# Delta heads of a hybrid decoder layer: PSUM banks shared out anew, and the weight sums' transfers placed elsewhere

## The chip, the cores and the metric

The kernel runs on one core of a Trainium2 chip. The metric is the time of one execution on the device in microseconds. A core has a matrix engine (TensorE, PE in the profile, with its weight loads as PEld), a vector engine (VectorE, DVE), a scalar engine (ScalarE, ACT) and a general one (GpSimd, POOL). SyncE (SP) only issues transfers (DMAs) here. Matmuls write to PSUM. In the stage that is changed the kernel's pools hold eight PSUM tiles of up to 2 KB in each of 128 partitions, one bank to a tile.

## The reference, cut to what matters

One layer over 512 tokens of width 2048, in float32. A projection feeds two branches: attention in a sliding window, and gated DeltaNet, a recurrence with one state S per head. Their outputs are gated, added and multiplied by `w_out`. DeltaNet has 16 key heads, 32 value heads (two to a key head) and heads of 128 channels.

```python
proj = h @ w_in
aq, ak, av, ag, d_qkv, dz, db, da, mg_a, mg_b = jnp.split(proj, _split_points(), axis=-1)
...
d_qkv = causal_conv_silu(d_qkv, conv_w)          # 4 taps
dq, dk, dv = jnp.split(d_qkv, [DN_KEY, 2 * DN_KEY], axis=-1)
...
o = gated_delta_rule(dq, dk, dv, g, beta)
o = rms_norm(o, dn_norm_w) * jax.nn.silu(dz.reshape(B, T, DN_V_HEADS, DN_HEAD_V).astype(f32))
y_b = o.reshape(B, T, DN_VAL).astype(x.dtype) @ w_o_dn
y = jax.nn.sigmoid(mg_a) * y_a + jax.nn.sigmoid(mg_b) * y_b
return x + gate * (y @ w_out)

def gated_delta_rule(q, k, v, g, beta):
    ...
    def step(S, xs):
        u_c, w_c, qk_c, qd_c, kd_c, gl_c = xs
        v_new = u_c - w_c @ S
        o = qd_c @ S + qk_c @ v_new
        S = S * gl_c[..., None, None] + jnp.swapaxes(kd_c, -1, -2) @ v_new
        return S, o
```

## The kernel before, in words

**Products.** A float32 product is made of three faster ones: both factors are split into a high and a low part, and `mm3` (L255 to L257) adds hi x hi, hi x lo and lo x hi in one PSUM tile of 128x512 (`mm`). For each half of a weight tile ACT casts the high part (`whi`, L61) and DVE subtracts for the low one (`wlo`, L62). A channel tile, 128 channels of the projection, is 16 such triples, 48 matmuls. The output products (of `w_od` and `w_out`) are made in a form with 7 block products instead of 8, which needs sums of weight blocks. Those sums are made early, by `weight_sums` (L1181), and stored in the DRAM tensors `g_d` and `f_d`: there are 24 sets, and each loads four tiles of 128x1024 (512 KB each; tags q00, q10, q11, q01, one buffer each; L1193), makes four sums on DVE (L1197) and stores them (L1199). A tile can be loaded anew only when the store that reads it has ended.

**Stages.** By the profile's times: start up to some 150 us, keys of DeltaNet and attention up to about 1066 us, the delta heads to about 2195 us, then the output products.

**Delta heads.** For each of the 16 key heads (a group g, `heads`, L802) five channel tiles are multiplied, 240 large matmuls: q, v0, v1, z0 and z1. Beside them runs the small work of the same group and the ones before:
- `values`: the conv (L604, then L609 and L611) gives `yv`, four transposes bring it to a PSUM tile `ptv`, and ACT copies that to `vt` (L829).
- `queries`: the conv gives `yq`, which is transposed (`ptq`). For each of two value heads a matrix of decays E is made: a row is loaded from `g_rows` (L737, on SP's queue), masked on POOL (L742), and put through exp on ACT (L748). Then come, each in a PSUM tile of the pool `ptph`: `pqk` (L884), `py` (L892, copied to Y by DVE) and two `pu` (L898 and L899).
- `scan` (L913): four steps c over blocks of 128 tokens. `pp` (L923) multiplies the state S by the keys; DVE makes `r` (L926); `pv` (L933) gives the new values, which ACT copies (`vn`, L935) and DVE scales (`vs`, L940); `pd` (L948) is the update of the state, `po` (L951, L952) the output. ACT copies `po` to `osb` (L953) and squares it twice for the norm (L956); DVE makes the new S from `pd` (L960 in the first step, L963 in the next ones). The next step's `pp` needs that S.
- the end of `scan`: DVE makes the norm (`ms`, the root, and `osb` times it, L982), PE transposes the two heads to `pto`, DVE multiplies that by the gates (`zh`, L989), and the results are stored in `o_d` (L993).

The small tiles `pp`, `pv`, `po` and `pd` come from the pool `psch`, the transposes, `pqk`, `py` and `pu` from `ptph`, the channel tiles from `pmmh`. A pool gives its buffers in turn; who writes a buffer next waits for the readers of what it held.

**What sets the order.** All of this is written as generators that are stepped by `pump` (L90), called once for each two triples, that is six matmuls. A generator started by `go` that yields n waits n pumps. One started by `paced` has a budget: so many units are added at each pump, and a yield of x costs x units. `behind` (L259) ties an instruction to the place of the last large matmul in the order, with no wait on the chip. A scheduler then fixes the order of each engine's instructions, which that engine works off one after the other. An instruction that waits holds up all that stand behind it on its engine. All DMAs are issued by SP, in one such order: weight loads (`raw`, L213), sums, rows of decays, results.

## Time and profile before

| | |
|---|---|
| median of 3 runs | 2892.16 us (2882.42 to 2896.01) |
| the profiled execution, its own time | 2893.1 us |
| its span in the profile | 2891.3 us |
| mean granted clock of TensorE | 0.995 |
| PE, delta heads (1066 to 2195 us): busy | 1113.63 of 1129.00 us, 5837 instructions |
| DVE, there | 731.21 us |
| ACT, there | 430.33 us |
| POOL, there | 78.16 us |
| bytes moved, there | 209 GB/s |

A row of the profile's groups of instructions gives the line, the engine, the operation, what is written and read (`out<-in`, buffer numbers left out), the shapes and the count, then the busy time with the mean of one in ns, then the idle time of the engine just before them and what ended it. A row of the waits view says who waited for whom: total, times, longest. A row of the timeline has the start, the length, the engine (SPq is SP's queue), the line, the instruction and, in brackets, the idle time before it with what ended it. A clock of 1.00 is TensorE's full speed.

### The profile page before, as it was taken

Reading aid. Unit: us, or ns where it says so; the run is one execution under the profiler, and the core shown is the slowest. Engines: PE = TensorE matmul, PEld = TensorE weight load, DVE = VectorE, ACT = ScalarE, POOL = GpSimd, SP = SyncE. Lnnn points to the kernel's source line nnn. Section 1 sums busy time; section 2 is a strip of 40 time slices with the busy share of each in tenths; the row PEclk is TensorE's granted clock in tenths of the full one; section 3 lists DMA queues with packets and bytes.
Section 4 is the critical chain, followed back from the end, with each engine's and each line's share of the span. In section 5 each row is a group of like instructions: output and inputs, shape, how many; then the busy total and the mean of one; then the engine's idle time right before and its main releaser. Section 6 shows DMA issues by size and latency. Waiting matters only on the chain.

```text
span 2891.3 us, 38617 instructions
## 1 busy us (share of the span) xinstructions
PE 2829.9 (98%) x14396; PEld 2320.6 (80%) x14396; DVE 1969.2 (68%) x3174; ACT 1189.4 (41%) x2382; POOL 138.4 (5%) x124
## 2 busy tenths in 40 slices
PE   7899999999999999999999999999999999999999
PEld 5687888877877778888788888888888788878887
DVE  6776786768768666767766666666656766664666
ACT  4356453334444343343433333333334444433343
POOL 0001010100001000100100000000000000000000
PEclk9999999999999999999999999999999999999999
DMA  9777774322252253335777677777746887885684
GB/s 383 292 256 223 242 248 142 114 89 86 83 158 82 108 161 129 121 111 174 255 260 243 233 245 252 241 237 248 242 151 221 279 307 264 298 278 175 245 318 166
DMA packets 227727, 604.27 MB, mean 209 GB/s; under 512 B 76082, under 2 KB 102194, under 8 KB 187090
## 3 DMA queue, kind: packets, MB, share of 16 engines
q1 hardware_dynamic: 227538, 601.81, 62.1%
q8 instruction: 113, 1.85, 0.3%
q14 instruction: 76, 0.61, 0.1%
HBM read 481.32 MB, written 118.17 MB: 207 GB/s over the span
## 4 chain that ended last, share of the span: by engine, by line
PE 84%; DMA 6%; DVE 5%; ACT 2%; issue 1%; POOL 0%; SPq 0%; DVEq 0%; POOLq 0%; ACTq 0%
PE mm L255 20%; PE mm L257 19%; PE mm L256 19%; PE m L256 5%; PE m L255 5%; PE m L257 5%; DMA g_d<-q 2%; DMA E<-g_rows 2%; DVE wlo L62 1%; PE S L1388 1%; DVE wa L437 1%; PE O L1439 1%; ACT whi L61 1%; PE pP L296 1%; PE pv L933 1%
## 5 line engine op out<-in xcount | busy, mean ns | idle before, releaser
L255 PE MATMUL mm<-hh,whi 128*128 128x512 f32 x2784 | 1132.3, 407 | 2.9 <-ACT mth L285 2.8
L257 PE MATMUL mm<-hh,wlo 128*128 128x512 f32 x2784 | 1091.5, 392 | 0.0
L256 PE MATMUL mm<-hl,whi 128*128 128x512 f32 x2784 | 1089.1, 391 | 0.0
L62 DVE TENSOR_TENSOR wlo<-raw,whi 128x1024 fp32r<-128x1024 f32 (+1 forms) x532 | 653.9, 1230 | 470.7 <-ACT whi L61 458.2
L61 ACT CAST whi<-raw 128x1024 fp32r<-128x1024 f32 (+1 forms) x532 | 555.3, 1045 | 867.1 <-PE mm L256 625.3
L255 PEld LDWEIGHTS mm<-hh,whi 128*128 128x128 f32 x2784 | 524.7, 188 | 114.6 <-issue 9.2
L257 PEld LDWEIGHTS mm<-hh,wlo 128*128 128x128 f32 x2784 | 523.7, 188 | 113.9 <-issue 0.5
L256 PEld LDWEIGHTS mm<-hl,whi 128*128 128x128 f32 x2784 | 525.2, 189 | 100.8 <-issue 1.4
L748 ACT ACTIVATE E<-E,neg_g 128x128 f32<-128x128 f32 x256 | 82.2, 393 | 103.5 <-POOL E L742 96.1
L1197 DVE TENSOR_TENSOR q<-q,q 128x1024 f32<-128x1024 f32 x96 | 121.0, 1261 | 0.1
L777 DVE TENSOR_TENSOR atmp<-A 128x62 f32<-128x62 f32 (+30 forms) x124 | 108.9, 878 | 0.5
L785 DVE TENSOR_TENSOR A<-A,atmp 128x62 f32<-128x62 f32 (+30 forms) x124 | 108.1, 872 | 0.5
L880 POOL TENSOR_TENSOR qe<-qe,yq 128x512 f32<-128x512 f32 x32 | 52.7, 1664 | 939.1 <-DMA qe<-eg_rows 809.0
L953 ACT COPY osb<-po 128x256 f32<-128x256 f32 x64 | 23.8, 372 | 153.0 <-PE po L952 153.0
L742 POOL TENSOR_SCALAR_AFFINE_SELECT E<-E 128x512 f32<-128x512 f32 x64 | 54.8, 868 | 448.4 <-DMA E<-g_rows 373.2
L1412 ACT ACTIVATE sm<-sm,mx,rs 128x256 f32<-128x256 f32 (+1 forms) x128 | 71.7, 562 | 3.5 <-DVE mx L1407 3.5
L935 ACT COPY vn<-pv 128x256 f32<-128x256 f32 x64 | 23.8, 372 | 119.5 <-PE pv L933 119.5
L604 DVE SCALAR_TENSOR_TENSOR yv<-mm,convh,yv 128x511 f32<-128x511 f32 (+2 forms) x96 | 71.1, 741 | 1.0
L940 DVE TENSOR_SCALAR vs<-vn,kd 128x128 f32<-128x128 f32 x96 | 23.1, 283 | 57.6 <-ACT vn L935 57.6
L926 DVE SCALAR_TENSOR_TENSOR r<-pp,neg_eg,vt 128x128 f32<-128x128 f32 x96 | 29.1, 344 | 40.6 <-PE pp L923 40.5
L437 DVE SCALAR_TENSOR_TENSOR wa<-wa,silu_cb 128x2048 f32<-128x2048 f32 x24 | 54.8, 2282 | 0.0
L952 PE MATMUL po<-vn,E 128*128 128x128 f32 x256 | 46.8, 275 | 0.0
(427 smaller groups left out, 3662.4 us busy)
## 6 DMA issues: line engine op xcount, KB each, us to landing
raw<-in_w_ch SPq DMA_DIRECT2D x158, 1024.0 KB
wa<-in_w_ada_ss SPq DMA_DIRECT2D x32, 1024.0 KB
q<-in_w_od SPq DMA_DIRECT2D x64, 512.0 KB
g_d<-q SPq DMA_DIRECT2D x64, 512.0 KB
raw<-g_d SPq DMA_DIRECT2D x32, 1024.0 KB
raw<-in_w_od SPq DMA_DIRECT2D x24, 1024.0 KB
gw<-in_w_ada_gate SPq DMA_DIRECT2D x16, 1024.0 KB
E<-g_rows SPq DMA_DIRECT2D x64, 256.0 KB
```

The source lines that it names most:

```text
L61: self.nc.scalar.copy(out=hi, in_=src)
L62: self.nc.vector.tensor_tensor(out=lo, in0=src, in1=hi.bitcast(F32), op=ALU.subtract)
L255: nc.tensor.matmul(ps, lhsT=wh, rhs=xh, start=first, stop=False)
L256: nc.tensor.matmul(ps, lhsT=wh, rhs=xl, start=False, stop=False)
L257: self.last_mm = nc.tensor.matmul(ps, lhsT=wl, rhs=xh, start=False, stop=last)
L437: nc.vector.scalar_tensor_tensor(out=wa, in0=wa, scalar=0.5, in1=scb, op0=ALU.mult, op1=ALU.mult, accum_out=t[:, j : j + 1])
L604: nc.vector.scalar_tensor_tensor(out=y[:, s:], in0=ps[:, : T - s], scalar=w[:, j : j + 1], in1=y[:, s:], op0=ALU.mult, op1=ALU.add)
L748: self.nc.scalar.activation(E[:, c, :], E[:, c, :], AF.Exp, bias=self.neg_g[:, c, h : h + 1])
L777: eng.tensor_tensor(out=t, in0=A[:, m : m + 1, m + 1 :].to_broadcast([P, m, n]), in1=A[:, :m, m : m + 1].to_broadcast([P, m, n]), op=ALU.mult,
L785: self.behind(eng.tensor_tensor(out=A[:, :m, m + 1 :], in0=A[:, :m, m + 1 :], in1=t, op=ALU.add))
L1197: self.behind(nc.vector.tensor_tensor(out=q[f], in0=q[x], in1=q[y], op=ALU.add))
L1412: nc.scalar.activation(t, t, AF.Exp, scale=r[:, h : h + 1], bias=mx[:, h : h + 1], accum_out=den[:, h : h + 1])
```

## The change

In `psch` three buffers stay of four, and `ptph` has three instead of two; the sum stays eight. `po` and `pd` become the two halves of one tile, `pod`. `pp` and `pv` are given the same size, and only half of each is used. The transposes `pto` are written one pump later (`yield 3`). The weight sums begin one group earlier, with 2.0 units per pump for 1.75. Each of their loads is tied to the last large matmul, with one unit between loads and 8.0 units behind the last; each sum is followed by 6.0 units for 4.0, the 2.0 units behind each store go, and 7.0 units stand behind a set. Lines from L1194 on stand one line further down in the changed kernel (the sums are L1198, their stores L1200).

```diff
--- before.py
+++ after.py
@@ -651,8 +651,8 @@
         tc, nc = self.tc, self.nc
         with ExitStack() as sb:
             self.pmm = sb.enter_context(tc.tile_pool(name="pmmh", bufs=2, space=PSUM, reuse_waits="tile"))
-            self.ptp = sb.enter_context(tc.tile_pool(name="ptph", bufs=2, space=PSUM, reuse_waits="tile"))
-            self.psc = sb.enter_context(tc.tile_pool(name="psch", bufs=4, space=PSUM, reuse_waits="tile"))
+            self.ptp = sb.enter_context(tc.tile_pool(name="ptph", bufs=3, space=PSUM, reuse_waits="tile"))
+            self.psc = sb.enter_context(tc.tile_pool(name="psch", bufs=3, space=PSUM, reuse_waits="tile"))
             self.gwk = sb.enter_context(tc.tile_pool(name="gwkh", bufs=1, reuse_waits="tile"))
             wk = sb.enter_context(tc.tile_pool(name="dnB", bufs=2, reuse_waits="tile"))
             self.tt = []
@@ -665,8 +665,8 @@
             ws = sb.enter_context(tc.tile_pool(name="wsum", bufs=1, reuse_waits="tile"))
             sums = None
             for g in range(KH):
-                if g == 4:
-                    sums = self.paced(self.weight_sums(ws), 1.75)
+                if g == 3:
+                    sums = self.paced(self.weight_sums(ws), 2.0)
                 if g == 8:
                     self.drain_slow(self.solves)
                 self.heads(wk, g)
@@ -919,7 +919,7 @@
         S = None
         for c in range(NTB):
             if c:
-                pp = self.psc.tile([P, 2, P], F32, tag="sc", name="pp")
+                pp = self.psc.tile([P, 4, P], F32, tag="sc", name="pp")[:, 0:2, :]
                 nc.tensor.matmul(pp, lhsT=kT[:, sl(c)], rhs=S, start=True, stop=True)
                 r = wk.tile([P, 2, P], F32, tag="r", name="r", bufs=1)
                 for e in range(2):
@@ -928,7 +928,7 @@
                         in1=v[e][:, c, :], op0=ALU.mult, op1=ALU.add,
                     )
                 yield 2
-            pv = self.psc.tile([P, 2, P], F32, tag="sc", name="pv")
+            pv = self.psc.tile([P, 4, P], F32, tag="sc", name="pv")[:, 0:2, :]
             for e in range(2):
                 nc.tensor.matmul(pv[:, e, :], lhsT=TT[e][:, c, :], rhs=r[:, e, :] if c else v[e][:, c, :], start=True, stop=True)
             vn = wk.tile([P, 2, P], F32, tag="vn", name="vn", bufs=2)
@@ -942,9 +942,9 @@
                         scalar2=None, op0=ALU.mult,
                     )
             yield 1
-            po = self.psc.tile([P, 2, P], F32, tag="sc", name="po")
+            pod = self.psc.tile([P, 4, P], F32, tag="sc", name="pod")
+            po, pd = pod[:, 0:2, :], pod[:, 2:4, :]
             if c < NTB - 1:
-                pd = self.psc.tile([P, 2, P], F32, tag="sc", name="pd")
                 nc.tensor.matmul(pd, lhsT=k[:, c, :], rhs=vs, start=True, stop=True)
             for e in range(2):
                 if c:
@@ -982,7 +982,7 @@
             nc.vector.tensor_tensor(
                 out=of, in0=of, in1=ro[:, e * NTB : (e + 1) * NTB].unsqueeze(2).to_broadcast([P, NTB, P]), op=ALU.mult
             )
-        yield 2
+        yield 3
         for e in range(2):
             pt = self.ptp.tile([P, T], F32, tag="tp", name="pto")
             self.transpose4(pt, lambda c: osb[:, e, c, :])
@@ -1190,14 +1190,15 @@
                         q = []
                         for c, r in ((0, 0), (1, 0), (1, 1), (0, 1)):
                             t = wk.tile([P, 1024], F32, tag=f"q{c}{r}", name=f"q{c}{r}", bufs=1)
-                            nc.sync.dma_start(out=t, in_=w[2 * c + n, 2 * r + i][:, cols])
+                            self.behind(nc.sync.dma_start(out=t, in_=w[2 * c + n, 2 * r + i][:, cols]))
                             q.append(t)
-                        yield 10.0
+                            yield 1.0
+                        yield 8.0
                         for f, (x, y) in enumerate(((0, 1), (1, 2), (0, 2), (2, 3))):
                             self.behind(nc.vector.tensor_tensor(out=q[f], in0=q[x], in1=q[y], op=ALU.add))
-                            yield 4.0
+                            yield 6.0
                             self.behind(nc.sync.dma_start(out=dst[n, f, i][:, cols], in_=q[f]))
-                            yield 2.0
+                        yield 7.0
 
     def rope_tables(self, wk, keep):
         nc, a = self.nc, self.a
```

DVE's order in the third step of the scan of group 11. `wlo` is half of a weight tile, `yq` the q tile of the next group; PE_49 and the like are semaphores of engines and of DMAs. Before:

```order
L940 TENSOR_SCALAR vs<-vn,kd 128x128 [waits Activation_49]
L940 TENSOR_SCALAR vs<-vn,kd 128x128
L62 TENSOR_TENSOR wlo<-raw,whi 128x1024 [waits DMAHW4_49,PE_49,Activation_49]
L963 SCALAR_TENSOR_TENSOR S<-S,egl,pd 128x128 [waits PE_49]
L963 SCALAR_TENSOR_TENSOR S<-S,egl,pd 128x128
L604 SCALAR_TENSOR_TENSOR yq<-mm,convh,yq 128x511 [waits Activation_49,Pool_49]
L604 SCALAR_TENSOR_TENSOR yq<-mm,convh,yq 128x510 [waits DVE_49]
L604 SCALAR_TENSOR_TENSOR yq<-mm,convh,yq 128x509 [waits DVE_49]
L611 SCALAR_TENSOR_TENSOR yq<-th,yq 128x512 [waits Activation_49]
L926 SCALAR_TENSOR_TENSOR r<-pp,neg_eg,vt 128x128 [waits PE_49]
```

The same place of the changed kernel:

```order
L940 TENSOR_SCALAR vs<-vn,kd 128x128 [waits DVE_49,Activation_49]
L940 TENSOR_SCALAR vs<-vn,kd 128x128
L62 TENSOR_TENSOR wlo<-raw,whi 128x1024 [waits DMAHW6_49,PE_49,Activation_49]
L604 SCALAR_TENSOR_TENSOR yq<-mm,convh,yq 128x511 [waits Activation_49,Pool_49]
L604 SCALAR_TENSOR_TENSOR yq<-mm,convh,yq 128x510 [waits DVE_49]
L604 SCALAR_TENSOR_TENSOR yq<-mm,convh,yq 128x509 [waits DVE_49]
L963 SCALAR_TENSOR_TENSOR S<-S,egl,pod 128x128 [waits PE_49,Activation_49]
L963 SCALAR_TENSOR_TENSOR S<-S,egl,pod 128x128
L611 SCALAR_TENSOR_TENSOR yq<-th,yq 128x512 [waits Activation_49]
L926 SCALAR_TENSOR_TENSOR r<-pp,neg_eg,vt 128x128 [waits PE_49]
```

S moved behind the three conv instructions, and it waits for ACT as well as for PE. In eight of the sixteen groups the third step reads so.

PE's order at `py`, group 5 (`lab` and `ta` are blocks from DRAM). Before:

```order
L256 MATMUL mm<-hl,whi 128x512
L257 MATMUL mm<-hh,wlo 128x512
L892 MATMUL py<-ta,lab 64x64 [waits DMAHW5_49,DMAHW4_49,Activation_49]
L892 MATMUL py<-ta,lab 64x64 [waits DMAHW2_49,DMAHW1_49]
L892 MATMUL py<-ta,lab 64x64 x6
L255 MATMUL mm<-hh,whi 128x512
```

The same place of the changed kernel:

```order
L256 MATMUL mm<-hl,whi 128x512
L257 MATMUL mm<-hh,wlo 128x512
L892 MATMUL py<-ta,lab 64x64 [waits DMAHW6_49,DMAHW0_49,DVE_49]
L892 MATMUL py<-ta,lab 64x64 [waits DMAHW2_49,DMAHW1_49]
L892 MATMUL py<-ta,lab 64x64 x6
L255 MATMUL mm<-hh,whi 128x512
```

Nothing moved; the engine that `py` waits for is DVE in place of ACT, since the bank that it takes held `pto` (read for `zh`) and not `ptv` (read for `vt`).

SP's order around the loads of E for group 6. Before:

```order
L859 DMA qe<-eg_rows 128x512 [waits DMAHW2_49,PE_49,Pool_49]
L1193 DMA q_12346<-in_w_od 128x1024 [waits DMAHW4_49,DMAHW3_49]
L1199 DMA g_d<-q_12026 128x1024 [waits DVE_49]
L1193 DMA q_12348<-in_w_od 128x1024 [waits DMAHW5_49,DMAHW0_49]
L737 DMA E<-g_rows 128x512 [waits DMAHW6_49]
L1193 DMA q_12350<-in_w_od 128x1024 [waits DMAHW7_49,DMAHW4_49]
L993 DMA o_d<-zh 128x512 [waits DVE_49]
L993 DMA o_d<-zh 128x512 [waits DMAHW1_49,DVE_49]
L213 DMA raw<-in_w_ch 128x2048 [waits DMAHW2_49,Activation_49]
L737 DMA E<-g_rows 128x512 [waits DMAHW3_49,PE_49]
```

The changed kernel:

```order
L865 DMA tt_9185<-ts_d 64x4x64 [waits DMAHW4_49,PE_49]
L213 DMA raw<-in_w_ch 128x2048 [waits DMAHW5_49,DVE_49]
L1200 DMA g_d<-q_12127 128x1024 [waits DMAHW6_49]
L859 DMA qe<-eg_rows 128x512 [waits DMAHW7_49,PE_49,Pool_49]
L859 DMA qe<-eg_rows 128x512 [waits DMAHW0_49,PE_49,Pool_49]
L737 DMA E<-g_rows 128x512 [waits DMAHW1_49]
L737 DMA E<-g_rows 128x512 [waits DMAHW2_49,PE_49]
L1200 DMA g_d<-q_12143 128x1024 [waits DMAHW3_49,DVE_49]
```

Both loads of E follow the loads of `qe`, where loads and stores of the sums and the stores of `zh` stood between.

## The prediction

> **What bounds the kernel now.** I read the page first, then the stages, then the waits of TensorE in the stage that the change touches.

> ```profile
> span 2891.3 us, 38617 instructions
> ...
> PE 2829.9 (98%) x14396; PEld 2320.6 (80%) x14396; DVE 1969.2 (68%) x3174; ACT 1189.4 (41%) x2382; POOL 138.4 (5%) x124
> ...
> L1197 DVE TENSOR_TENSOR q<-q,q 128x1024 f32<-128x1024 f32 x96 | 121.0, 1261 | 0.1
> ```

> TensorE is busy for 98% of the span, so it is the bound, and what it does is not changed: no matmul goes or comes. The change can only move the time in which TensorE waits, and the time in which it runs at a lower clock. The stages view of the delta heads (1066 to 2195 us) and of two places in it says how much there is (columns: stretch, its length, busy time of PE, PEld, DVE, ACT and POOL with counts, granted clock, DMA share, GB/s):

> ```profile
> 1066.00:2195.00 1129.00, 1113.63 (x5837) 926.01 (x5835) 731.21 (x1187) 430.33 (x997) 78.16 (x62) 1.00 0.64 209
> 1440.00:1445.00 5.00, 2.76 (x12) 1.90 (x11) 4.18 (x4) 2.62 (x6) 2.35 (x1) 1.00 0.99 379
> 1445.00:1450.00 5.00, 4.30 (x24) 3.51 (x25) 3.08 (x4) 1.92 (x6) 0.64 (x1) 0.50 1.13 384
> 1450.00:1455.00 5.00, 5.00 (x32) 3.75 (x31) 2.25 (x5) 1.68 (x2) 0.00 (x0) 0.81 0.87 244
> 1917.00:1922.00 5.00, 4.43 (x24) 3.74 (x25) 5.00 (x7) 2.00 (x5) 0.00 (x0) 1.00 0.27 104
> ```

> PE is idle for 1129.0 - 1113.6 = 15.4 us of this stage. At 1445 the clock falls to half and stays there into the next stretch: 5 x 0.50 + 5 x 0.19 = 3.4 us of work are lost, though PE counts as busy. In the last row, where PE waited too, it stays at 1.00. Who was waited for (total us, times, longest), from 1070 to 2190 us:

> ```profile
> PE py L892 <- ACT vt L829: 5.5, 3, 2.9
> PE pto L296 <- DVE osb L982: 4.4, 3, 2.1
> PE ptv L296 <- DVE yv L611: 2.0, 2, 1.3
> PE ptv L296 <- DVE zh L989: 1.9, 1, 1.9
> PE pv L933 <- DVE r L926: 0.4, 1, 0.4
> PE pp L923 <- DVE S L963: 0.2, 1, 0.2
> ```

> That is 14.4 us of waits, and 17.8 us with the lower clock: 0.6% of the kernel. This is the most that the change can win where it works. The longest wait, in order of time, on SP's queue, POOL, ACT and PE (start, length, instruction, idle time before it):

> ```profile
> 1433.28 0.33 SPq L1193 DMA_DIRECT2D q<-in_w_od  x1
> 1433.66 0.45 SPq L737 DMA_DIRECT2D E<-g_rows  x1
> ...
> 1439.02 3.33 POOL L742 TENSOR_SCALAR_AFFINE_SELECT E<-E 128x512 f32<-128x512 f32 x1 [1.45 <-DMA E<-g_rows]
> 1442.38 1.28 ACT L748 ACTIVATE E<-E,neg_g 128x128 f32<-128x128 f32 x4 [8.67 <-POOL E L742]
> ...
> 1443.57 1.03 ACT L61 CAST whi<-raw 128x1024 fp32r<-128x1024 f32 x1
> ...
> 1445.08 0.56 ACT L829 COPY vt<-ptv 128x512 f32<-128x512 f32 x1
> 1445.70 1.11 PE L892 MATMUL py<-ta,lab 64*64 64x64 f32 x15 [2.94 <-ACT vt L829]
> ```

> The rows of decays (E), issued right behind a load of the weight sums, land 5 us later; POOL waits for them, ACT 8.67 us for POOL, and behind ACT's exponentials stand a cast and the copy vt, which frees the bank that py is to write. PE needs nothing of the late E here (it belongs to the next group); it waits for a bank. And SP's queue, which issues E, is late itself:

> ```profile
> SPq L1193 <- DMA g_d<-q: 113.1, 37, 8.1
> SPq L1199 <- DVE q L1197: 82.5, 38, 7.4
> SPq L1193 <- DMA f_d<-q: 57.0, 17, 7.2
> ```

> Loads of the weight sums wait on SP, up to 8.1 us each, until the store that still reads their tile has ended, and all that stands behind them waits too.

> **The change part by part.** *Third bank (ptph 2 to 3).* In the order of before, py waits for ACT; in the changed order it waits for DVE, that is for zh, two transposes earlier. The waits of 5.5 us go, and the lower clock that follows the longest of them: 5.5 + 3.4 = 8.9 us. The cover is the next user of a bank, pu, 12 matmuls later, which now waits for vt. From 1899.88 to 1900.11 (rows below) a matmul takes 0.23 us, so vt has 12 x 0.23 = 2.8 us more, against a longest wait of 2.9. If E lands as late as at 1439, the win of that one wait is near its 2.8 us all the same, but if it comes later, pu waits instead; ends of this term: 3 to 8.9 us. I take 8.9, since the loads of E also come forward.

> *Sums held behind the matmuls and spread.* The loads of a set come 7 units of 2.0 per pump after its last store, 3.5 pumps, where there were 2 units of 1.75; a pump is six matmuls, 6 x 0.23 = 1.4 us, so the last store has 4.8 us before the next loads begin, where it had 2 / 1.75 x 1.4 = 1.6 us. SP mostly finds its tiles free. In the changed order both E stand straight behind qe in most groups; the second E for group 10 still stands behind the stores of zh, and those of three groups behind one store of sums. The 96 sums on DVE (1261 ns each) and the 192 DMAs stay as many. By itself this is the cure of the late E; its worth is in the other terms.

> *One pump more before pto (yield 3).* The three waits of 4.4 us are those in which sums and casts stand inside the chain of small instructions before osb:

> ```profile
> 1909.61 1.23 DVE L1197 TENSOR_TENSOR q<-q,q 128x1024 f32<-128x1024 f32 x1
> 1910.83 1.22 DVE L62 TENSOR_TENSOR wlo<-raw,whi 128x1024 fp32r<-128x1024 f32 x1
> 1916.82 1.29 DVE L982 TENSOR_TENSOR osb<-osb,roy 128x512 f32<-128x512 f32 x2
> 1917.57 0.66 PE L296 MATMUL pto<-ident,osb 128*128 128x128 f32 x4 [2.09 <-DVE osb L982]
> ```

> A pump of 1.4 us covers the two shorter ones (2.3 us together) and 1.4 of the 2.1: 3.7 us; all 4.4 where no sum (1.2 us) falls into the chain. I take 4.2. What was hidden behind the transposes, the stores of o_d, moves by 1.4 us; nobody but SP's order waits for them.

> *The waits of ptv.* The rows of the two longest:

> ```profile
> 1235.28 0.63 PE L296 MATMUL ptv<-ident,yv 128*128 128x128 f32 x4 [1.35 <-DVE yv L611]
> ...
> 1648.60 0.68 DVE L611 SCALAR_TENSOR_TENSOR yv<-th,yv 128x512 f32<-128x512 f32 x1
> 1649.20 0.68 DVE L989 TENSOR_TENSOR zh<-pto,zh 128x512 f32<-128x512 f32 x1
> ```

> The 1.9 us were spent on the second zh, which ptv no longer needs: it needs yv, 0.6 us earlier. Of the 2.0 us for yv, 1.3 lie at 1235 us, where no sum was made yet, and stay. I leave two waits of 0.7 us (2.0 - 1.3) more or less as they are: 3.9 us become 2.7, 1.2 us won. The ends: 0, and 2.6 if only the 1.3 is left.

> *One bank for po and pd.* This is the part that can cost. The state S (DVE) may now read its half only after ACT has read the other half three times, and its wait stands ahead of wlo, r and the conv on DVE's queue. The third step of a scan, now:

> ```profile
> 1896.23 0.60 PE L948 MATMUL pd<-vs,k 128*128 128x256 f32 x2
> 1899.88 0.39 PE L256 MATMUL mm<-hl,whi 128*128 128x512 f32 x1
> 1900.11 0.39 PE L257 MATMUL mm<-hh,wlo 128*128 128x512 f32 x1
> 1900.34 0.59 PE L923 MATMUL pp<-S,kT 128*128 128x256 f32 x2
> 1895.93 1.22 DVE L62 TENSOR_TENSOR wlo<-raw,whi 128x1024 fp32r<-128x1024 f32 x1 [1.35 <-ACT whi L61]
> 1897.07 0.60 DVE L963 SCALAR_TENSOR_TENSOR S<-S,egl,pd 128x128 f32<-128x128 f32 x2
> 1897.59 2.31 DVE L604 SCALAR_TENSOR_TENSOR yq<-mm,convh,yq 128x511 f32<-128x511 f32 x3
> 1898.61 0.19 ACT L956 ACTIVATION_READ_ACCUMULATOR junk<-po 128x1 f32 x1
> ```

> ACT is done at 1898.61 + 0.19 = 1898.80; S could end at 1899.40, and pp wants it at 1900.34: 0.9 us to spare. But in eight of the sixteen groups the changed order puts all three conv instructions ahead of S here. They would start at 1897.07 and end at 1899.38; S ends 0.60 later, at 1899.98. So 0.36 us are left, less what a signal takes; say 0.3. I take 0 for the term. The ends: nothing, or one wlo more (1.2 us) ahead of S in the third steps of 15 groups, 15 x (1.2 - 0.3) = 14 us. [...]

> The sum: 8.9 + 4.2 + 1.2 = 14.3 us. The profiled execution took 2893.1 us, 1.8 more than its span, and the median of the three runs is 2892.2, so no correction is needed: 2893.1 - 14.3 = 2878.8, say 2879 us, 0.46% less. With the better ends of the terms for pto and ptv (4.4 and 2.6) it is 2877, with the worse ones (3.7 and 0) 2881; 2 us either way for the scatter make the forecast's own bounds 2875 to 2883.

> **The rivals.** *E stays late.* The loads of the sums still stand ahead of some E, 2 MB of them, and E lands behind them; the waits of py move to pu or ptv. For it: the row at 1433.66, right behind one such load. Against: most E stand before them now. Left is pto (4.2) and 3 of the 8.9: 2893 - 7 = 2886.

> *The scan pays.* The 14 us above are paid: 2893, no change. It decides at 0.3 us of delay in the third step. Against it: of the 48 states that pp needs (three to a group), one came late so far, by 0.2 us (the waits of PE).

> *All waits go.* 17.8 us and no residue: 2875.

> *A sum waits for its load, slower than before.* The loads are no longer issued far ahead: the first sum of a set comes 5.5 pumps, 7.6 us, behind the second load, which it needs. A sum that waits holds DVE, and behind it S, r and wlo. There are 24 sets (96 sums, four to a set); past the 0.9 us to spare each costs what it waits. At 2.2 us: 24 x 1.3 = 31 us, 2879 + 31 = 2910; it makes the kernel slower by over 0.5% from 2.1 us on. For it: a store of 512 KB was waited for up to 8.1 us. Against: SP runs ahead of the place at which a load is written, and the sums waited 0.1 us in all so far (first view).

> *The clock.* With three banks for a scan instead of four, short waits follow each other; if one in each group brought the clock down as at 1445, 16 x 3.4 = 54 us: 2879 + 54 = 2933. Against: after the wait of 2.09 the clock stayed at 1.00, and over the whole stage its mean is 1.00. [...]

> **How the numbers follow.** The forecast (2875 to 2883) has 0.58, E late 0.13, the scan pays 0.08, all waits go 0.09, a sum waits 0.08, the clock 0.04. A measurement of this kernel tells about 0.5% from no change, 14.5 us, so the line is at 2878 us, inside the forecast's own bounds. I put half of that case on each side: faster 0.29 + 0.09 = 0.38; the same 0.29 + 0.13 + 0.08 = 0.50; slower 0.08 + 0.04 = 0.12. The range goes from 2872 (all waits gone, and 3 us for the scatter of the runs, which lay between 2882 and 2896) to 2892, and leaves out the slower cases and half of the scan's.

> **What would show it.** Right: in the waits of PE no row py from vt and none for pto over 1 us, the clock at 1.00 in every stretch of the heads, the SP row "L1193 <- DMA g_d<-q" far below 113 us, PE busy unchanged within 4 us. Wrong: new rows "pp <- S" or "pu <- vt" of several us, a row of DVE in which the sum waits for a DMA, or a second fall of the clock.

## The result, and the profile after

The changed kernel takes 2872.93 us in the median of 8 runs (2871.02 to 2877.28). Over 8 runs the kernel before has a median of 2887.82 us, so the ratio is 0.9946, with a 95% interval from 0.9934 to 0.9958. That is 14.9 us less. The forecast was 2879 us, 14.3 us less than the execution that it started from; 2872.93 lies below the forecast's own bounds of 2875 to 2883 and inside the stated range, 2872 to 2892. First the page of the changed kernel's profiled execution (2872.0 us), then the stages view of the delta heads, before and after, from the first matmul of the stage to the first one behind it:

```profile
span 2870.2 us, 38671 instructions
...
PE 2820.4 (98%) x14396; PEld 2314.6 (81%) x14396; DVE 1969.6 (69%) x3174; ACT 1188.4 (41%) x2382; POOL 141.6 (5%) x124
```

```profile
1064.89:2195.56 1130.67, 1114.74 (x5840) 926.95 (x5841) 732.84 (x1189) 431.13 (x999) 78.16 (x62) 1.00 0.64 209
```

```profile
1060.10:2176.38 1116.28, 1110.47 (x5841) 924.74 (x5841) 733.83 (x1189) 431.17 (x999) 80.47 (x62) 1.00 0.63 212
```

The stage is 14.39 us shorter, with the same work on every engine. The two spans differ by 21.1 us, but 4.8 of that lie ahead of the stage (it starts at 1060.10 for 1064.89) and 1.9 behind it, where nothing was changed; the last section comes back to the 4.8. What follows compares the stage. The waits of PE in it, after the change:

```profile
PE pv L933 <- DVE r L926: 2.5, 1, 2.5
PE ptv L296 <- DVE yv L611: 0.7, 1, 0.7
PE pu L898 <- DVE Y L894: 0.6, 1, 0.6
PE pod L948 <- DVE vs L940: 0.3, 1, 0.3
PE pp L923 <- DVE S L960: 0.2, 1, 0.2
```

They sum to 4.3 us, for 14.4. The rows of py and pto are gone, and so is the half clock in the stage (3.4 us): 10.1 + 3.4 = 13.5 of the 14.4 us. One of the signs named for being right did not come: PE's busy time was to stay within 4 us, and it fell by 9.5 us on the page and by 4.3 us in the stage, because the time at half clock counts as busy (before, from 1445 to 1450 us, 4.30 of 5.00 us at a clock of 0.50). On SP's queue the loads of the sums wait far less for their stores (the stores wait longer for the sums, 107.8 us for 82.5):

```profile
SPq L1200 <- DVE q L1198: 107.8, 40, 6.2
...
SPq L1193 <- DMA g_d<-q: 25.6, 8, 4.9
SPq L1193 <- DMA f_d<-q: 6.9, 2, 4.8
```

The part that could cost is the state in the shared bank. The third step of the same scan as in the prediction (start, length, instruction):

```profile
1880.22 0.60 PE L948 MATMUL pod<-vs,k 128*128 128x256 f32 x2
...
1881.05 2.31 DVE L604 SCALAR_TENSOR_TENSOR yq<-mm,convh,yq 128x511 f32<-128x511 f32 x3
...
1882.59 0.19 ACT L956 ACTIVATION_READ_ACCUMULATOR junk<-pod 128x1 f32 x1
...
1883.28 0.60 DVE L963 SCALAR_TENSOR_TENSOR S<-S,egl,pod 128x128 f32<-128x128 f32 x2
...
1884.32 0.59 PE L923 MATMUL pp<-S,kT 128*128 128x256 f32 x2
```

ACT is done with the bank at 1882.78, the three conv instructions on DVE end at 1883.36, S ends at 1883.88 and pp starts at 1884.32: 0.44 us to spare. Where no conv stands ahead of S, 0.87 to 0.90 us are left in most groups (1.08 in most first steps). With a bank of its own the state had 2.40 to 2.86 us in nearly all steps of the kernel before, so the change took 1.3 to 2.2 us of room, and it cost next to nothing: pp waited once in 48 steps, 0.2 us.

The longest wait that is left:

```profile
1400.25 2.02 ACT L790 COPY atmp<-A 64x1024 f32<-64x1024 f32 x1 [2.50 <-DMA ta_d<-atmp]
...
1402.18 1.04 ACT L61 CAST whi<-raw 128x1024 fp32r<-128x1024 f32 x1
...
1403.25 1.22 DVE L62 TENSOR_TENSOR wlo<-raw,whi 128x1024 fp32r<-128x1024 f32 x1 [4.86 <-ACT whi L61]
1404.39 0.60 DVE L926 SCALAR_TENSOR_TENSOR r<-pp,neg_eg,vt 128x128 f32<-128x128 f32 x2
...
1404.79 0.75 PE L933 MATMUL pv<-r,tt 128*128 128x128 f32 x4 [2.49 <-DVE r L926]
```

A copy of the triangular solves holds ACT for 2 us, the cast behind it comes late, wlo behind that, and r stands behind wlo in DVE's order.

### The profile page after: what moved, and what is told of

Same layout as the page of the kernel before. It is cut to its first block, busy times and chain, and to the rows that moved or that the text cites. A ratio compares the mean times of both kernels' runs of the same rounds, so it can differ in the third digit from the quotient of the medians.

```text
span 2870.2 us, 38671 instructions
## 1 busy us (share of the span) xinstructions
PE 2820.4 (98%) x14396; PEld 2314.6 (81%) x14396; DVE 1969.6 (69%) x3174; ACT 1188.4 (41%) x2382; POOL 141.6 (5%) x124
## 4 chain that ended last, share of the span: by engine, by line
PE 87%; DVE 5%; DMA 3%; ACT 2%; issue 1%; SPq 0%; POOL 0%; DVEq 0%; POOLq 0%; ACTq 0%
PE mm L255 20%; PE mm L257 20%; PE mm L256 20%; PE m L256 5%; PE m L255 5%; PE m L257 5%; DVE wa L437 1%; DVE wlo L62 1%; PE pv L933 1%; DMA E<-g_rows 1%; PE S L1389 1%; PE pod L952 1%; PE O L1440 1%; PE pP L296 1%; ACT sm L1413 1%
## 5 line engine op out<-in xcount | busy, mean ns | idle before, releaser
L257 PE MATMUL mm<-hh,wlo 128*128 128x512 f32 x2784 | 1089.5, 391 | 0.0
L256 PE MATMUL mm<-hl,whi 128*128 128x512 f32 x2784 | 1086.9, 390 | 0.0
L62 DVE TENSOR_TENSOR wlo<-raw,whi 128x1024 fp32r<-128x1024 f32 (+1 forms) x532 | 655.2, 1232 | 425.0 <-ACT whi L61 409.6
L61 ACT CAST whi<-raw 128x1024 fp32r<-128x1024 f32 (+1 forms) x532 | 555.4, 1045 | 848.6 <-PE mm L256 612.2
L257 PEld LDWEIGHTS mm<-hh,wlo 128*128 128x128 f32 x2784 | 522.6, 188 | 113.6 <-issue 0.5
L256 PEld LDWEIGHTS mm<-hl,whi 128*128 128x128 f32 x2784 | 524.0, 188 | 100.4 <-issue 1.4
L1198 DVE TENSOR_TENSOR q<-q,q 128x1024 f32<-128x1024 f32 x96 | 124.5, 1297 | 0.2 <-DMA q<-in_w_od 0.2
L748 ACT ACTIVATE E<-E,neg_g 128x128 f32<-128x128 f32 x256 | 82.1, 393 | 88.7 <-POOL E L742 88.6
L953 ACT COPY osb<-pod 128x256 f32<-128x256 f32 x64 | 23.8, 372 | 149.9 <-PE pod L952 149.9
L742 POOL TENSOR_SCALAR_AFFINE_SELECT E<-E 128x512 f32<-128x512 f32 x64 | 60.0, 950 | 430.7 <-DMA E<-g_rows 307.2
L604 DVE SCALAR_TENSOR_TENSOR yv<-mm,convh,yv 128x511 f32<-128x511 f32 (+2 forms) x96 | 71.4, 743 | 1.2
L963 DVE SCALAR_TENSOR_TENSOR S<-S,egl,pod 128x128 f32<-128x128 f32 x64 | 19.3, 343 | 50.8 <-ACT junk L956 50.8
L609 ACT ACTIVATE th<-yv 128x512 f32<-128x512 f32 x32 | 20.1, 628 | 72.7 <-DVE yv L604 72.7
```

What stands on the lines that cost most here:

```text
L61: self.nc.scalar.copy(out=hi, in_=src)
L62: self.nc.vector.tensor_tensor(out=lo, in0=src, in1=hi.bitcast(F32), op=ALU.subtract)
L256: nc.tensor.matmul(ps, lhsT=wh, rhs=xl, start=False, stop=False)
L257: self.last_mm = nc.tensor.matmul(ps, lhsT=wl, rhs=xh, start=False, stop=last)
L604: nc.vector.scalar_tensor_tensor(out=y[:, s:], in0=ps[:, : T - s], scalar=w[:, j : j + 1], in1=y[:, s:], op0=ALU.mult, op1=ALU.add)
L748: self.nc.scalar.activation(E[:, c, :], E[:, c, :], AF.Exp, bias=self.neg_g[:, c, h : h + 1])
```

## The experiments

All are read by the length of the stage of the heads, from its first matmul to the first one behind it. The table gives that length, PE's waits in it (between 1070 and 2170 us), the work lost to the half clock there, and the measured median. Each ratio is to executions of the kernel before that were taken beside it (medians of 2887.8 to 2888.4 us). A stage's length comes from one profiled execution, and the whole times of these lie up to 6 us from their medians, so a difference of a few us between two stages is shown only where the runs agree with it.

| kernel | stage us | waits | half clock | median us | ratio (95% interval) |
|---|---|---|---|---|---|
| before | 1130.7 | 14.4 | 3.4 | 2887.82 | 1 |
| the change | 1116.3 | 4.3 | 0 | 2872.93 | 0.9946 (0.9934 to 0.9958) |
| sums only | 1119.1 | 5.3 | 1.7 | 2873.21 | 0.9951 (0.9935 to 0.9967) |
| banks only | 1123.3 | 8.8 | 1.7 | 2880.15 | 0.9967 (0.9957 to 0.9978) |
| pump only | 1150.7 | 28.3 | 8.5 | 2902.18 | 1.0043 (1.0030 to 1.0056) |
| sums and banks | 1120.7 | 7.0 | 1.7 | 2876.33 | 0.9956 (0.9939 to 0.9974) |
| sums and pump | 1129.2 | 13.9 | 1.7 | 2887.35 | 0.9998 (0.9987 to 1.0009) |
| rhythm, loads untied | 1117.3 | 4.3 | 0 | 2876.39 | 0.9956 (0.9943 to 0.9970) |
| loads tied, old rhythm | 1124.2 | 10.6 | 1.7 | 2880.39 | 0.9973 (0.9961 to 0.9984) |
| change, sums 4 pumps later | 1128.5 | 14.1 | 1.7 | 2888.95 | 0.9998 (0.9986 to 1.0009) |
| change, sums 6 pumps later | 1115.0 | 3.9 | 0 | 2872.75 | 0.9947 (0.9929 to 0.9964) |
| change, copies on POOL | 1118.4 | 5.0 | 1.7 | 2875.88 | 0.9959 (0.9944 to 0.9974) |

### The parts one by one

The sums alone, that is this part of the change on the kernel before:

```diff
-                if g == 4:
-                    sums = self.paced(self.weight_sums(ws), 1.75)
+                if g == 3:
+                    sums = self.paced(self.weight_sums(ws), 2.0)
...
+                            yield 1.0
+                        yield 8.0
...
-                            yield 4.0
+                            yield 6.0
...
+                        yield 7.0
```

> Only the weight sums are placed as in the change; banks and the pump are as before. Theory A, the prediction's: each part has its own term, and the sums alone are worth little: py still waits for vt by 3 us or more, pto for osb by about 4.4, PE's waits in the heads stay at 12 to 14 us, ratio 0.998 to 1.000. Theory B: the late E, and sums that stand in the way, are the source of nearly all, and their new places alone take it away: waits in the heads at most 5 us, ratio 0.994 to 0.997.

```profile
PE ptv L296 <- DVE yv L611: 2.6, 3, 1.7
PE pv L933 <- DVE r L926: 2.4, 1, 2.4
PE pd L948 <- DVE vs L940: 0.3, 1, 0.3
```

Neither py nor pto waits, with two banks in ptph and without the pump. Theory A falls: the sums alone bring 11.6 of the stage's 14.4 us. By the runs they can't be told from the whole change at all (2873.21 and 2872.93 us).

The banks alone:

```diff
-            self.ptp = sb.enter_context(tc.tile_pool(name="ptph", bufs=2, space=PSUM, reuse_waits="tile"))
-            self.psc = sb.enter_context(tc.tile_pool(name="psch", bufs=4, space=PSUM, reuse_waits="tile"))
+            self.ptp = sb.enter_context(tc.tile_pool(name="ptph", bufs=3, space=PSUM, reuse_waits="tile"))
+            self.psc = sb.enter_context(tc.tile_pool(name="psch", bufs=3, space=PSUM, reuse_waits="tile"))
...
+            pod = self.psc.tile([P, 4, P], F32, tag="sc", name="pod")
+            po, pd = pod[:, 0:2, :], pod[:, 2:4, :]
```

> Only the banks (third for ptph, three for psch, po and pd in one tile); the sums and the pump are as before. Theory A: the row py from vt is gone and the half clock with it, pto (4.4) and ptv (about 3.9) stay: about 9 us less, ratio 0.996 to 0.998. Theory B: E is as late as before and the wait for vt moves to pu or ptv, with a row of 3 us or more: ratio 0.998 to 1.000.

The row of py is gone here too, pto stays at 4.5, ptv at 2.6, and pp (1.1) and pu (0.6) are new. 7.4 us of the stage were won. By themselves the banks do about what the prediction said (7.4 us for 8.9); they are no use for what the sums already took away, as the next run shows.

The change without the pump (`yield 2` ahead of pto, as before), so sums and banks:

> The change without the pump ahead of pto (yield 2). Theory A: the row pto from osb is back at 3.5 to 4.4 us, ratio about 0.996. Theory B: pto waits under 1.5 us, since the sums lie elsewhere, ratio 0.9946 as the whole change.

pto waits once, 0.8 us, ptv 3.2 and pv 2.7. Of the two theories that is B's row for pto; but the stage is 4.4 us longer than the change's, 2.7 by waits and 1.7 by a half clock. The runs don't confirm that difference: their intervals overlap (0.9939 to 0.9974, and 0.9934 to 0.9958). The stage is 1.6 us longer than with the sums alone: on top of the sums the banks bring nothing.

The change without the banks, so sums and pump:

> The change without the banks: two for ptph, four for psch, po and pd apart; sums and pump as in the change. Theory A: py waits for vt by 3 to 5.5 us again, ratio 0.997 to 0.998. Theory B: py waits under 1 us, since E comes in time; ratio about 0.9946 as the whole change.

```profile
PE ptv L296 <- DVE zh L989: 7.8, 8, 1.2
PE pv L933 <- DVE r L926: 2.8, 1, 2.8
PE py L892 <- ACT vt L829: 2.3, 1, 2.3
```

Neither theory had this: the gain is gone, and the largest row is a new one. One of its eight places:

```profile
1438.08 0.69 DVE L989 TENSOR_TENSOR zh<-pto,zh 128x512 f32<-128x512 f32 x1
...
1438.82 0.66 PE L296 MATMUL ptv<-ident,yv 128*128 128x128 f32 x4 [1.04 <-DVE zh L989]
```

With two banks, ptv takes the one that pto held; the pump moves pto and zh 1.4 us later and ptv stays where it is, so ptv waits about 1 us. With three banks it takes another one. So the pump does harm without the bank. Next the pump alone, on the kernel before:

```diff
-        yield 2
+        yield 3
```

> Only the pump ahead of pto (yield 3), the rest as before. If the pump is worth its own 4.2 us, as the prediction had it, the row pto from osb is gone and the ratio is about 0.998. If it needs the third bank, as the run without banks suggests (ptv waited 7.8 us in 8 waits for zh there), a row ptv from zh of 6 to 10 us stands in its place and the ratio is 1.001 to 1.004.

```profile
PE ptv L296 <- DVE zh L989: 11.3, 8, 3.4
PE pqk L884 <- DVE zh L989: 5.8, 5, 2.8
PE pto L296 <- DVE osb L982: 4.4, 3, 2.1
PE py L892 <- ACT vt L829: 3.8, 3, 1.9
PE py L892 <- DMA o_d<-zh: 3.0, 1, 3.0
```

It is slower than before by 0.43%, 12 us by the runs and 20 us in the stage of the profiled execution, which is the slowest of its five. pto waits as before: 4.4 us, 3 times, in the same three groups (3, 11 and 14). Alone, the pump doesn't cure that wait, since osb comes later too: from the first ms to the end of the first osb it takes 10.0 us in group 3 and 9.7 in group 11, where it took 7.9 and 9.0 before. The pump's worth depends on the bank: by the stage +20.0 us alone, +10.1 on top of the sums, -4.4 on top of sums and banks. The loss without the bank is clear of the scatter of the runs; the gain with it is not.

### What of the sums does it

Three theories: the gap between a store and the next load of its tile (C), the tie of the loads to the matmuls (D), or merely the places that the sums come to stand in (E). The new rhythm with untied loads:

```diff
-                            self.behind(nc.sync.dma_start(out=t, in_=w[2 * c + n, 2 * r + i][:, cols]))
+                            nc.sync.dma_start(out=t, in_=w[2 * c + n, 2 * r + i][:, cols])
                             q.append(t)
-                            yield 1.0
-                        yield 8.0
+                        yield 12.0
```

> Banks and pump as before; the sums in the new rhythm (one group earlier, 2.0 per pump, 6.0 units behind each sum, 7.0 behind a set), but the four loads of a set are written together and not tied to the last large matmul. Theory C, the gap: what counts is the time between a store and the next load of its tile; SP no longer waits in the loads for stores, E is issued in time, waits of PE in the heads 5 to 8 us, ratio 0.994 to 0.997 as with the new places alone. Theory D, the tie: what counts is the place of the loads; untied they stand far ahead in SP's order, wait there for their stores, E stays late: waits 12 us or more, ratio 0.998 to 1.000.

```profile
SPq L1193 <- DMA g_d<-q: 144.3, 43, 9.1
SPq L1193 <- DMA f_d<-q: 81.0, 17, 8.0
```

The waits are those that C forecast, but not by C's way: SP waits longer for stores than before (113.1 and 57.0), and E comes late in several groups. PE hardly sees it (py waits once, 1.6 us). One such place, on ACT, and the py that runs there:

```profile
1365.12 0.59 ACT L829 COPY vt<-ptv 128x512 f32<-128x512 f32 x1
...
1373.57 1.28 ACT L748 ACTIVATE E<-E,neg_g 128x128 f32<-128x128 f32 x4 [0.31 <-POOL E L742]
```

```profile
1367.79 0.68 PE L892 MATMUL py<-ta,lab 64*64 64x64 f32 x16
```

The exponentials of the late E stand behind vt in ACT's order here, and hold up nothing. In the row at 1442.38 of the kernel before they stood ahead of vt (1445.08). The one wait of py here is of that kind too: E at 1702.90, vt at 1706.77, py at 1707.39. All eleven waits of py in the fourteen profiles are of this kind (the row of 3.0 us of the pump alone, put down to a DMA, among them: vt ended at 1445.97 and py began at 1446.02). A late E cost something only where ACT's order has it ahead of vt.

The tie with the old rhythm (group 4, 1.75 per pump, no gap; in place of the `yield 10.0` four times `yield 1.0` and `yield 6.0`):

> Banks and pump as before; the four loads of a set are tied to the last large matmul with one unit between them, but the rhythm is that of before (group 4, 1.75 per pump, no gap behind a set). Theory C, the gap: the loads still wait for the stores on SP (over 100 us in that row), E stays late, waits of PE in the heads 12 us or more, ratio 0.998 to 1.000. Theory D, the tie: E comes in time and the waits are 5 to 8 us, ratio 0.994 to 0.997.

SP's rows fell to 52.3 and 9.0 us, so the tie does relieve SP. But pto waits 5.9 us in 3 waits and py 2.6 in 2 (there again E stands ahead of vt): the stage has 6.4 of the 14.4 us, about half of the gain. C and D both fall as the cause of the whole. What sets pto apart is seen in DVE's order between the last `ms` of a scan and `osb`. How many sums and conv instructions stand there, by group from 0 to 15:

```
before                       0 0 0 1+3 0 0 0 0 0 0 0 1+3 0 0 1+3 0
the change                   0 0 0 0 0 0 0 0 0 0 0 0 0 0 0 0
change, sums 4 pumps later   0 0 2+3 2+3 2+3 0 0 0 1+3 2+3 2+3 2+3 0 0 0 0
change, sums 6 pumps later   0 0 0 0 0 0 0 0 0 0 0 0 0 0 0 0
```

In the kernel before, pto waited in groups 3, 11 and 14. Banks only, pump only and the tied loads in the old rhythm have the row of before, and pto waits in the same three groups; sums only, sums and pump and the untied loads have the change's row, and no row for pto. The two shifted kernels have the change's rhythm, banks and pump, and one line more ahead of the first set:

```diff
         sets = [(a["w_od"][0], self.g_d[0]), (a["w_od"][1], self.g_d[1]), (a["w_out"], self.f_d)]
+        yield 8.0
         for w, dst in sets:
```

> The whole change, with one yield of 8 units (4 pumps) ahead of the first set: the same rhythm, all sums 4 pumps later. In the order of DVE two sums and three conv instructions now stand between ms and osb in six groups, one sum and the conv in a seventh; in the change there is none. Theory E, the phase: what the sums cost is set by where they fall. That chain took 4.55 us without and 8.5 to 9.2 us with one sum and three conv in the profile before, so about 10 us with two; pto has 2.8 us of room: 6 x 2.7 + 1.5 = 18 us of waits for osb, and ratio 1.000 to 1.005. Theory C, the gap (room between a store and the next load), or D, the tie: both are as in the change, ratio 0.993 to 0.996.

> As the run before, with 12 units (6 pumps): in the order no sum stands between ms and osb in any group. Theory E, the phase: no row pto from osb over 1 us, ratio 0.993 to 0.996, as the change. If a shift costs for another reason than this chain (the end of the stage, the last sums), the ratio is above 0.998 here too.

The sums 4 pumps later:

```profile
PE pto L296 <- DVE osb L982: 11.0, 8, 2.0
```

```profile
1900.57 0.16 DVE L975 SCALAR_TENSOR_TENSOR ms<-osq,epsq 128x4 f32<-128x4 f32 x1 [0.23 <-ACT junk L956]
...
1901.26 1.22 DVE L1199 TENSOR_TENSOR q<-q,q 128x1024 f32<-128x1024 f32 x1
...
1903.76 0.74 DVE L604 SCALAR_TENSOR_TENSOR yv<-mm,convh,yv 128x511 f32<-128x511 f32 x1
...
1906.27 1.21 DVE L1199 TENSOR_TENSOR q<-q,q 128x1024 f32<-128x1024 f32 x1
...
1908.96 1.29 DVE L982 TENSOR_TENSOR osb<-osb,roy 128x512 f32<-128x512 f32 x2
```

The same chain in the change:

```profile
1892.87 0.16 DVE L975 SCALAR_TENSOR_TENSOR ms<-osq,epsq 128x4 f32<-128x4 f32 x1 [0.23 <-ACT junk L956]
...
1896.13 1.29 DVE L982 TENSOR_TENSOR osb<-osb,roy 128x512 f32<-128x512 f32 x2
...
1900.21 0.60 PE L296 MATMUL pto<-ident,osb 128*128 128x128 f32 x4
```

From `ms` to the end of `osb` it takes 4.55 us in the change and 9.7 with two sums in it, and pto has 2.8 us of room. Four pumps take back the whole gain (0.9998), six take back nothing (0.9947). E holds for the waits of pto. The 18 us forecast for pto were 11.0: pto needs only the first of the two `osb` (0.6 us earlier), and the waits were 1.4 to 2.0 us each in most groups. The median of this kernel is 6 us above its profiled execution (2882.95 us, the fastest of its runs), so most of its runs lose more than this profile shows. Part of that may lie ahead of the stage: in this execution the heads start at 1057.3 us, earlier than in any other profile.

### The price of the shared bank

The first try made each square three times in every step:

```diff
-                nc.scalar.activation(junk, po[:, e, :], AF.Square, accum_out=osq[:, e, c : c + 1])
+                for _ in range(3):
+                    nc.scalar.activation(junk, po[:, e, :], AF.Square, accum_out=osq[:, e, c : c + 1])
```

> The change with each of the two squares of the norm made three times in every step of the scan, four more reads of pod by ACT ahead of S (the results are the same). They take about 0.33 us each, 1.3 us in all. If the room of the state is as the profile of the change has it (1.05 us in the first step, 0.87 in the second and 0.44 in eight third steps), pp waits for S in nearly all of 48 steps, 16 x 0.3 + 24 x 0.45 + 8 x 0.9 = 23 us, and ratio to before is about 1.002 to 1.005. If S is not held by the bank or the room is wider, pp waits under 5 us and the ratio stays near 0.995.

It took 2944.37 us, ratio 1.0188 (1.0170 to 1.0205), and pp waited only 3.4 us. The test missed its question: the order had changed. pp stands 14 to 23 large matmuls behind pod there, not 12, the scan ends later, and pto waits 40.5 us in 16 waits. So the second try made the squares three times in the first three steps only, and tied the ten triples written behind pp to it, so that most pp keep their place:

```diff
-        nc.tensor.matmul(ps, lhsT=wh, rhs=xh, start=first, stop=False)
+        ms = [
+            nc.tensor.matmul(ps, lhsT=wh, rhs=xh, start=first, stop=False),
...
+        if getattr(self, "pin", None) is not None:
+            for m in ms:
+                self.behind(m, self.pin)
...
-                nc.tensor.matmul(pp, lhsT=kT[:, sl(c)], rhs=S, start=True, stop=True)
+                self.left = 10
+                self.pin = nc.tensor.matmul(pp, lhsT=kT[:, sl(c)], rhs=S, start=True, stop=True)
...
+                for _ in range(3 if c < NTB - 1 else 1):
```

> The change with each square made three times in the first three steps of the scan, and the large matmuls behind pp held back until pp, so that pp keeps its place 12 large matmuls behind pod in 34 of 48 steps (15 or 16 in 14 third steps, which have some 0.7 to 0.9 us more room so). Four more reads of pod, about 1.3 us. If the room of the state is 1.05 us (first step) and 0.87 (second): 16 x 0.3 + 16 x 0.45 = 12 us of waits of pp for S, the third steps near nothing; ratio 0.998 to 1.001. If the scan had more room than that, under 3 us of such waits and a ratio below 0.9965.

```profile
PE pp L933 <- DVE S L974: 28.4, 18, 3.5
PE pp L933 <- DVE S L971: 8.9, 16, 2.7
```

It took 2942.18 us, ratio 1.0184 (1.0163 to 1.0204). In 15 of the 16 groups the first step waits 0.41 us (forecast 0.3) and the second 1.56 (forecast 0.45); the third waits in two groups, 0.7 us. The second step is 1.1 us longer than forecast since a cast of 1.0 us stands between the squares on ACT there (at 1130.05 us, for one). So the room of the state is as read, about 1 us, and what goes beyond it is paid in every group. The stage grew by 70 us in all; the waits account for 48 (not all of them for S: ptv and pto wait 12.6 us), half clocks for 10, and 12 stay unexplained.

### A try at more

The wait of 2.5 us for r follows on a copy of the solves. The change with those copies on POOL (the edit moves all eight; four lie in this stage):

```diff
-            nc.scalar.copy(out=t, in_=A[:HD, :, q * 16 : (q + 1) * 16].rearrange("u j i -> u i j"))
+            nc.gpsimd.tensor_copy(out=t, in_=A[:HD, :, q * 16 : (q + 1) * 16].rearrange("u j i -> u i j"))
```

> The change with the four copies of the second batch of solves (L790, 2.0 us each on ACT) made by POOL. The longest wait that is left, pv for r (2.5 us at 1405 us), and pod for vs (0.3) follow on such a copy, which holds the next cast on ACT. If so, both rows go, 2.8 us, ratio about 0.9936. If the cast was late for another reason, or POOL's copies hold up the masks of E, the row stays or another of 2 us or more comes, and the ratio is 0.9946 or above.

```profile
PE pu L898 <- DVE Y L894: 2.0, 1, 2.0
PE pp L923 <- DVE S L960: 1.3, 1, 1.3
PE ptv L296 <- DVE yv L611: 1.1, 1, 1.1
```

The rows of pv and pod are gone, as forecast, but others of 2.0 and 1.3 us come, with a half clock, and the stage is 2.1 us longer than the change's. No kernel here is measurably faster than the change.

## Why the prediction was right in its number, and wrong in its parts

*Third bank, 8.9 us.* The waits of py did go, and with the old sums the bank alone gives 7.4 us of the stage. But with the new sums py has no wait left to cure (sums only). In the change's profile the third bank covers one late vt: it is copied from 1640.12 to 1640.68, and py started at 1639.83, so about 0.9 us. The step that failed is "I take 8.9, since the loads of E also come forward": that is two cures for the same 5.5 us and the half clock behind it, and the term was booked on the one that was needed less.

*Sums, "its worth is in the other terms".* This is the step that failed most. The sums alone take 11.6 us off the stage. They are the main cause, in two ways. The 4.4 us of pto hang on where the 96 sums stand in DVE's order: that is shown by the shifts, and by the same three groups in four kernels. The 5.5 us of py, and the half clock behind the longest wait, come only where E stands late ahead of vt on ACT; whether the sums alone cure this by an earlier E or by another order on ACT was not separated. By the runs nothing is left for banks and pump together on top of the sums (2873.21 and 2872.93 us).

*One pump, 4.2 us.* By the stage its share was -4.4 us on top of sums and banks: the size was met by chance, since there was only 0.8 us of pto left to cure, and the runs don't show the gain clear of their scatter. The step "a pump of 1.4 us covers the two shorter ones" failed: alone, pto waits 4.4 us as before, and the later zh makes ptv and pqk wait 17.1 us. "Nobody but SP's order waits for them" overlooked that zh also frees the bank of pto. What I had seen for py, that a bank's last reader counts, I didn't ask of the step that the change delays.

*ptv, 1.2 us.* 3.9 us became 0.7, so 3.2 were won. The 1.3 at 1235 us, which was to stay, went too.

*The shared bank, 0.* Right: 0.3 us of room behind three conv and 0.9 without were forecast from the row, 0.44 and 0.87 were found, with one wait of 0.2. No run shows that S could not have read its half sooner. What the profiles show is that it did wait for ACT: 65.6 us in 29 waits of the stage after the change stood until ACT's squares were done, where before it waited for pd alone (19.4 us, 16 times). The rival "the scan pays" was worked out on that wait. Its 14 us did not come, and the second run with squares shows that it is real beyond about 1 us (28.4 and 8.9 us of pp for S).

*The other rivals.* E late: it comes late once (group 10) and costs nothing. A sum that waits for its load: it did so once, 0.2 us, and no wait of PE came of it. The clock: no fall in the stage after the change, and the short waits one after the other that it took are not there (in the scan PE waited three times, 2.5, 0.3 and 0.2 us). All waits go: 4.3 us stayed.

*The time.* 2879 was 14.3 less than an execution of 2893.1; the 8 runs put the kernel before at 2887.82, so the forecast was 6.1 us high, 5.3 of them by its starting point, and right in the difference, 14.3 for 14.9. That the parts sum up so well is luck: taken one by one they change the stage by -11.6, -7.4 and +20.0, together +1.0, where the whole brings -14.4.

## What to carry to other kernels

Where several edits aim at the same wait, price each of them with the others in place: here two cured the same wait, and a third did harm without one of them (ratio 1.0043 alone). Ask of a step that is delayed which buffer its last reader frees, and who takes that next. Background work on DVE, which works off one fixed order, cost here by where it fell: count in the order what stands inside each chain that PE waits for, and try shifts (here the sums 4 pumps later gave a ratio of 0.9998, 6 pumps later 0.9947), before changing the rhythm or the buffers.

## What the runs showed of the hardware

The half clock came after some waits and not after others. In the profiles of the twelve kernels of the table it fell 12 times in the stage, always at or just behind a wait of PE of 1.9 us or more, for 3.4 or 6.8 us. Of 16 waits of 2.0 to 3.4 us, 10 brought it; the change's 2.49 us didn't, while 2.41 us at the same place with the sums alone did. What differs between these two is how the wait lies in time. In every profile all steps of the clock lie whole multiples of 3.41 us apart. Cut into windows of that length, the change's wait is split between two of them, and the other lies nearly whole in one. The change, then the sums alone (the second number is the length, the third PE's busy time, and the clock is third from the end):

```profile
1400.28:1403.69 3.41, 2.02 (x9) 1.31 (x7) 0.44 (x1) 2.93 (x2) 0.00 (x0) 1.00 0.26 87
1403.69:1407.11 3.42, 2.32 (x12) 2.02 (x13) 1.79 (x5) 0.76 (x2) 0.00 (x0) 1.00 1.00 196
```

```profile
1403.29:1406.71 3.42, 1.13 (x5) 0.58 (x4) 1.42 (x3) 1.97 (x2) 0.00 (x0) 1.00 0.38 78
1406.71:1410.12 3.41, 3.29 (x10) 2.81 (x11) 0.81 (x4) 0.37 (x1) 0.00 (x0) 0.50 0.92 220
```

The start of the kernel runs in two ways. The first 60 us, before and after, with the clock in the third column from the end:

```profile
0.00:60.00 60.00, 42.72 (x305) 35.95 (x306) 39.90 (x99) 25.85 (x35) 0.21 (x4) 0.91 0.98 394
```

```profile
0.00:60.00 60.00, 42.27 (x314) 35.60 (x314) 41.87 (x103) 27.98 (x38) 0.21 (x4) 0.97 0.98 401
```

The code ahead of the heads is the same in all fourteen profiles, but for the copies of the solves in the last kernel. In the seven with one fall of the clock in the first 50 us the heads start at 1057.3 to 1060.1 us, in the seven with two falls at 1060.1 to 1066.1. The clock first reaches full speed at 13.7 to 14.5 us in the former and at 14.8 to 16.4 us in the latter, so the two ways go with where the windows of 3.41 us lie against the start of the kernel; that this is the cause is not shown. Single spans differ by up to 9 us before the change is even reached, so a stage's length says more than a span.
